# The second ring of moving tiles, laid 128 bytes further in SBUF

## The chip, the cores and the metric

The kernel runs on one core of one Trainium2 chip. The metric is the device time of one execution in microseconds (us). TensorE (PE) multiplies, VectorE (DVE) and ScalarE (ACT) work elementwise, GpSimd (POOL) does a few small steps, SyncE (SP) issues the DMAs. SBUF is the on-chip memory in which the operands lie: 128 partitions, each with its own bytes, so that a tile has a first byte within the partition.

## The reference

One layer of a decoder trunk over 2048 tokens of width 1024: a mixer of two head groups, an MLP with squared ReLU, and a gated embedding. The change touches what lies behind the mixer groups:

```python
mix = jnp.concatenate([o_a..., o_b...], axis=-1)
h = h + rms_norm(einsum('btc,cd->btd', mix, w_out), post_mix_norm)      # output projection
u = einsum('btd,df->btf', rms_norm(h, pre_mlp_norm), w_mlp_up)          # up: 1024 -> 4096
y = einsum('btf,fd->btd', square(relu(u)), w_mlp_down)                  # down: 4096 -> 1024
h = h + rms_norm(y, post_mlp_norm)
e = rms_norm(einsum('bte,ed->btd', p, w_ple_proj), ple_norm)
h = h + e * sigmoid(einsum('btd,de->bte', h, w_ple_gate))               # gate
```

All arrays are float32.

## The kernel before

**Matmuls.** Everything is held transposed: features on the partitions, tokens along them, in blocks of 512 tokens (q = 0 to 3). A float32 operand is split into two parts, high and low, of the type that TensorE reads in one pass (split, line 157: ACT copies the high part, DVE subtracts it from the original). A product takes three matmuls of 128x512 for each 128 rows: high by high, high by low, low by high. The weights, 128x128, are loaded into TensorE for each matmul; the other operand, 128x512, moves through it. So one matmul reads its moving operand from SBUF while the weights of the next are read from there.

**Stages.** Up to about 1145 us the input projection and the two mixers run (line 1020 and the lines around it). Behind them come the output projection (products named mmo, four token blocks of 8 products with 24 matmuls each), the MLP in two halves of two token blocks each (up, products named u; then down, products named d), and the gate (products named mmg). Up and down use a Strassen scheme: seven products in place of eight, with sums of tiles made by DVE. In up a group of 7 products has 12 matmuls each, 84 together, and there are 16 groups in each half. These products run through mm (line 1085) and, all but those of the down stage, through product (line 1092), which goes to the next moving tile and the next block of weights after three matmuls. The down stage (line 1540) uses one moving tile with four blocks of weights, 12 matmuls, before it goes on. Lines 1085 to 1090 also run the agenda: every 8 matmuls one step of the work that was put off (loads, splits, norms, residuals), so that this work goes with the matmuls.

**Pools.** A pool is a stretch of SBUF, cut into buffers. Pools of the left side lie one behind the other in the order in which they are opened, those of the right side from the top down. What matters here, with the buffers of each:

- left, for the whole kernel: cp (small constants), ra (10 buffers of 4096 bytes a partition), st (norms' tiles), sm (small tiles)
- left, closed before the stages behind the mixers: the mixers' pools cm, mp, m2
- left, opened in their place: pad (one tile that nothing uses), rb (18 buffers of 4096 bytes), f2 (16 buffers of 2048 bytes: results, sums and raw weights), tp (4 buffers of 2048 bytes)
- right: wp (weights: 3 buffers of 8192 and 2 of 4096 bytes), up to the first group of the up stage
- right, opened in the place of wp and tp: bp (10 buffers of 4096 bytes: weights of the up stage and the gate; both operands of the down stage)

The moving tiles of the output projection, the up stage and the gate (mixT, t, h2T) lie in the ring that ra and rb form together; next_pool deals them out. Of each 28 tiles the first 10 lie in ra, the others in rb:

```python
    def next_pool():
        turn[0] += 1
        return ra if (turn[0] - 1) % 28 < 10 else second[0]
```

Each such tile is 128 partitions by 2 parts of 512 float32, so 4096 bytes a partition; a buffer of weights has parts of 128 columns, 512 bytes. The tiles are taken in this order: mixT of token blocks 0 to 3 (8 each), 28 of the up stage's first half, 28 of its second, h2T of token blocks 0 to 3 (8 each). The moving tiles of the input projection all lie in ra, those of the down stage in bp.

Of the kernel before, what the change touches and what calls it, by code (L numbers as in the profile page):

```python
# [10 lines left out]
F32 = mybir.dt.float32  # L11
# [9 lines left out]
P = 128  # L21
# [62 lines left out]
def trunk(ctx, tc, x, xT, pT, vecs, w_in, w_ab, gdn_a_log, gdn_dt_bias, w_out, w_up, w_down,  # L84
# [986 lines left out]

    ctx.enter_context(tc.tile_pool(name="pad", bufs=1)).tile([P, 16], F32, name="pad")
    second.append(ctx.enter_context(tc.tile_pool(name="rb", bufs=18, reuse_waits="tile")))
    f2 = ctx.enter_context(tc.tile_pool(name="f2", bufs=1, reuse_waits="tile"))
    octx = ctx.enter_context(ExitStack())
# [656 lines left out]
```

## Time and profile before

| what | us |
|---|---|
| median of 3 runs | 2773.16 |
| lowest and highest | 2772.43, 2774.76 |
| profiled execution | 2769.21 |
| its span | 2767.3 |

The span runs from the first to the last instruction on the engines; the profiled execution's own time has what lies around it as well. The profile's page gives each engine's busy time, the chain of work that ended last, and groups of instructions by line, with count, busy time and mean length of one. For a stretch of time, a window gives the same busy times and counts. In order of time, a row gives the start, the length from the first to the end of the last, and the count of a run of like instructions. Matmuls overlap: one lasts some 390 ns from its first read to its last write, but the next starts well before that.

### The profile page before, as it was taken

The page shows a single profiled execution, that of the slowest core. Times are in us where ns is not written, and L with a number is a line of the kernel's source. Part 1 is how long each engine was busy: PE and PEld are TensorE (multiplying, and loading weights), DVE is VectorE, ACT ScalarE, POOL GpSimd, SP SyncE. Part 2 cuts the span into 40 slices and gives each one's busy share as a digit, 9 for nine tenths or more (in the row PEclk, how much of TensorE's full clock was granted, in tenths as well). Part 3 has the DMA queues.
Part 4 walks back from the last instruction along what each step waited for, and adds up shares of the span by engine and source line. Part 5 has one row for each costly group of instructions (what it writes and reads, how often), then busy time and mean ns, then how long its engine had stood idle before and what let it go on. Part 6 is the DMA issues. An engine that isn't in the chain of part 4 may idle for free.

```text
span 2767.3 us, 38374 instructions
## 1 busy us (share of the span) xinstructions
PE 2680.7 (97%) x12721; PEld 2215.3 (80%) x12721; DVE 2044.9 (74%) x4242; ACT 1469.9 (53%) x2943; POOL 104.2 (4%) x104
## 2 busy tenths in 40 slices
PE   6999999999999999999999999999999999999999
PEld 4788788788888887777788888887888888887887
DVE  6788877787787677578889867857787765567775
ACT  6665555455546445575555646545454445465431
POOL 0000000000000000000000000001000000001000
PEclk9999999999999999999999999999999999999999
DMA  7776777667666665887466447667454356577663
GB/s 261 255 250 217 235 247 247 219 209 250 220 213 202 214 227 170 278 276 258 140 214 224 172 175 237 225 193 239 157 191 162 135 175 203 194 254 240 214 206 121
DMA packets 268598, 589.24 MB, mean 213 GB/s; under 512 B 55642, under 2 KB 59960, under 8 KB 249200
## 3 DMA queue, kind: packets, MB, share of 16 engines
q1 hardware_dynamic: 268400, 586.79, 63.6%
q8 instruction: 101, 1.65, 0.3%
q14 instruction: 97, 0.79, 0.1%
HBM read 419.75 MB, written 166.92 MB: 212 GB/s over the span
## 4 chain that ended last, share of the span: by engine, by line
PE 61%; DVE 15%; DMA 10%; issue 7%; ACT 4%; SPq 1%; POOL 1%; DVEq 0%; POOLq 0%; ACTq 0%
PE u L1090 22%; PE d L1090 20%; PE mm L1020 9%; PE mmg L1090 6%; DVE pr_g L658 2%; DMA ud_g<-u_g 2%; DMA sys_g<-ud_g 2%; DVE xs_g L661 1%; DVE xs_g L663 1%; PE mmo L1090 1%; DMA raw_out<-in_w_out_dram 1%; DVE xt L160 1%; DMA rd_g<-m_g 1%; DMA cache_in<-w 1%; DMA rsb_g<-rd_g 1%
## 5 line engine op out<-in xcount | busy, mean ns | idle before, releaser
L1020 PE MATMUL mm<-xt,w 128*128 128x512 f32 x3072 | 770.0, 399 | 3.3 <-ACT qk_h L758 1.6
L1020 PEld LDWEIGHTS mm<-xt,w 128*128 128x128 f32 x3072 | 559.5, 189 | 109.8 <-ACT qk_h L758 2.0
L1090 PE MATMUL d<-db,da 128*128 128x512 f32 x2688 | 615.3, 391 | 5.6 <-ACT db L212 3.7
L1090 PE MATMUL u<-t,wu 128*128 128x512 f32 x2604 | 603.7, 393 | 3.3 <-ACT wu L159 3.3
L1090 PEld LDWEIGHTS d<-db,da 128*128 128x128 f32 x2688 | 506.3, 189 | 113.9 <-ACT db L212 5.0
L1090 PEld LDWEIGHTS u<-t,wu 128*128 128x128 f32 x2604 | 488.7, 188 | 117.6 <-ACT wu L159 4.1
L213 DVE TENSOR_TENSOR db<-db 128x512 fp32r<-128x512 f32 x224 | 161.4, 720 | 75.2 <-ACT db L212 74.3
L1419 DVE TENSOR_TENSOR u<-u,u 128x512 f32<-128x512 f32 x224 | 150.3, 682 | 71.8 <-PE u L1090 70.6
L212 ACT ACTIVATE db<-db 128x512 fp32r<-128x512 f32 x224 | 140.8, 629 | 83.2 <-DMA db<-hid 77.8
L1090 PE MATMUL mmo<-mixT,w_out 128*128 128x512 f32 x720 | 171.7, 399 | 8.9 <-DVE w_out L160 6.4
L1090 PE MATMUL mmg<-h2T,wg 128*128 128x512 f32 x768 | 177.4, 393 | 0.0
L1460 ACT ACTIVATE u<-u 128x512 f32<-128x512 f32 x128 | 80.8, 632 | 176.4 <-DVE u L1419 176.1
L1090 PEld LDWEIGHTS mmo<-mixT,w_out 128*128 128x128 f32 x720 | 137.1, 191 | 42.5 <-DVE w_out L160 8.2
L1090 PEld LDWEIGHTS mmg<-h2T,wg 128*128 128x128 f32 x768 | 144.2, 188 | 32.9
L160 DVE TENSOR_TENSOR da<-da 128x512 fp32r<-128x512 f32 x128 | 93.0, 727 | 87.1 <-ACT da L159 86.9
L159 ACT ACTIVATE da<-da 128x512 fp32r<-128x512 f32 x128 | 80.4, 628 | 134.9 <-DMA da<-sumd 111.3
L159 ACT ACTIVATE wu<-a 128x512 fp32r<-128x512 f32 x124 | 73.9, 622 | 50.6 <-DMA a<-in_w_up_dram 49.2
L658 DVE TENSOR_TENSOR pr_g<-xs_g,sys_g 128x16 f32<-128x16 f32 (+14 forms) x240 | 93.8, 391 | 5.3
L223 POOL TENSOR_TENSOR acc_y<-acc_y,sq_y 128x512 f32<-128x512 f32 x28 | 38.5, 1374 | 1392.8 <-ACT sq_y L222 1392.0
L160 DVE TENSOR_TENSOR wu<-a,wu 128x512 fp32r<-128x512 f32 x124 | 84.7, 686 | 3.6 <-ACT wu L159 3.5
L1461 ACT ACTIVATE u<-u 128x512 f32<-128x512 f32 x128 | 80.8, 631 | 3.7
L160 DVE TENSOR_TENSOR da<-dr,da 128x512 fp32r<-128x512 f32 x96 | 66.2, 690 | 18.5 <-ACT da L159 16.8
(374 smaller groups left out, 3800.9 us busy)
## 6 DMA issues: line engine op xcount, KB each, us to landing
w<-cache_in SPq DMA_DIRECT2D x96, 1024.0 KB
db<-hid SPq DMA_DIRECT2D x224, 256.0 KB
cache_in<-w SPq DMA_DIRECT2D x32, 1024.0 KB
hid<-u SPq DMA_DIRECT2D x128, 256.0 KB
da<-sumd SPq DMA_DIRECT2D x128, 256.0 KB
a<-in_w_up_dram SPq DMA_DIRECT2D x124, 256.0 KB
hid<-ht SPq DMA_DIRECT2D x96, 256.0 KB
dr<-in_w_down_dram SPq DMA_DIRECT2D x96, 256.0 KB
```

Source lines behind the costliest of these rows:

```text
L159: S.activation(t[:, 0], raw, AF.Copy)
L160: eng.tensor_tensor(t[:, 1], raw, t[:, 0], ALU.subtract)
L212: S.activation(t[:, 0], plain(t), AF.Copy)
L213: V.tensor_tensor(t[:, 1], plain(t), t[:, 0], ALU.subtract)
L223: eng.tensor_tensor(acc, acc, sq, ALU.add)
L658: V.tensor_tensor(pr[:, :, :, 0:i], xs[:, None, :, 0:i].broadcast_to([P, 2, GC, i]), sys[:, 0:i, i : i + 2].rearrange("p j two -> p two j" ...
L661: V.tensor_reduce(xs[:, :, i : i + 2].rearrange("p g two -> p two g"), pr[:, :, :, 0 : i + 1], AX.X, ALU.add)
L1020: PE.matmul(ps, *terms[i], start=i == 0, stop=i == nt - 1)
L1090: PE.matmul(ps, a, b, start=start, stop=stop)
L1419: V.tensor_tensor(c[new], c[old], ps, ALU.add)
L1460: S.activation(c[k], c[k], AF.Relu)
L1461: S.activation(c[k], c[k], AF.Square)
```

## The change

The tile in the pool pad, which is there only to take up room, grows from 16 to 48 float32, from 64 to 192 bytes a partition. The pools that are opened behind it on the left side, rb, f2 and tp, begin 128 bytes higher. No instruction, no order and no buffer count is changed.

```diff
@@ -1071,7 +1071,7 @@
-    ctx.enter_context(tc.tile_pool(name="pad", bufs=1)).tile([P, 16], F32, name="pad")
+    ctx.enter_context(tc.tile_pool(name="pad", bufs=1)).tile([P, 48], F32, name="pad")
     second.append(ctx.enter_context(tc.tile_pool(name="rb", bufs=18, reuse_waits="tile")))
     f2 = ctx.enter_context(tc.tile_pool(name="f2", bufs=1, reuse_waits="tile"))
     octx = ctx.enter_context(ExitStack())
```

## The prediction

> **What bounds the kernel now.** I read the page's busy shares and its chain first, then the windows of the stages behind the mixers, then the order of time of TensorE alone.
>
> ```profile
> span 2767.3 us, 38374 instructions
> ...
> PE 2680.7 (97%) x12721; PEld 2215.3 (80%) x12721; DVE 2044.9 (74%) x4242; ACT 1469.9 (53%) x2943; POOL 104.2 (4%) x104
> ...
> PE 61%; DVE 15%; DMA 10%; issue 7%; ACT 4%; SPq 1%; POOL 1%; DVEq 0%; POOLq 0%; ACTq 0%
> PE u L1090 22%; PE d L1090 20%; PE mm L1020 9%; PE mmg L1090 6%; DVE pr_g L658 2%; DMA ud_g<-u_g 2%; DMA sys_g<-ud_g 2%; DVE xs_g L661 1%; DVE xs_g L663 1%; PE mmo L1090 1%; DMA raw_out<-in_w_out_dram 1%; DVE xt L160 1%; DMA rd_g<-m_g 1%; DMA cache_in<-w 1%; DMA rsb_g<-rd_g 1%
> ```
>
> TensorE (PE) is busy for 97% and most of the chain is its matmuls of line 1090. The change touches only what is laid out behind the mixers, from about 1145 us on, so the stages from there are what counts: output projection (mmo), MLP up (u), MLP down (d), gate (mmg).
>
> ```profile
> 1145.00:1180.00 35.00, 33.94 (x149) 27.47 (x147) 14.37 (x20) 15.36 (x26) 2.02 (x2) 1.00 0.88 301
> 1180.00:1225.00 45.00, 44.84 (x192) 35.96 (x192) 36.88 (x53) 34.72 (x54) 0.00 (x0) 1.00 0.87 289
> 1225.00:1285.00 60.00, 52.37 (x209) 41.30 (x209) 49.77 (x75) 37.11 (x57) 0.00 (x0) 0.94 0.70 230
> 1285.00:1327.00 42.00, 42.00 (x184) 34.28 (x183) 34.90 (x56) 28.03 (x46) 0.00 (x0) 1.00 0.75 259
> 1327.00:1362.00 35.00, 29.37 (x113) 22.08 (x111) 23.69 (x39) 16.50 (x26) 0.00 (x0) 0.90 0.27 88
> 1362.00:1650.00 288.00, 286.78 (x1238) 232.55 (x1239) 235.21 (x379) 159.46 (x267) 0.00 (x0) 1.00 0.56 194
> ...
> 1962.00:2273.00 311.00, 310.85 (x1347) 252.40 (x1346) 231.51 (x366) 158.23 (x262) 5.83 (x4) 1.00 0.45 157
> 2273.00:2583.00 310.00, 307.57 (x1349) 253.72 (x1347) 196.55 (x293) 162.23 (x262) 13.27 (x10) 0.99 0.69 224
> 2583.00:2761.00 178.00, 178.00 (x772) 144.45 (x770) 125.11 (x191) 51.96 (x85) 5.44 (x4) 1.00 0.55 180
> ```
>
> Columns: window, length, then busy time and count of PE, its weight loads, DVE, ACT and POOL, granted clock, DMA share, GB/s. Both up stages (1362:1650, 1962:2273) and the gate (2583:2761) have TensorE busy practically without a gap at a clock of 1.00; DVE has 53 of 288 us free in the first of them. There every ns of a matmul is a ns of the kernel. From 1145 to 1362 us it isn't so: gaps, and a clock of 0.94 and 0.90.
>
> **What differs between the tiles.** Busy time hides what a matmul costs, because one is already running when the next starts. What I need is the step from start to start: (length of a gapless stretch less the last matmul's own 0.39 us) divided by (count less one). The rows below are TensorE in order of time; each is start, length, group, count.
>
> ```profile
> 1145.63 26.68 PE L1090 MATMUL mmo<-mixT,w_out 128*128 128x512 f32 x117
> 1237.10 11.08 PE L1090 MATMUL mmo<-mixT,w_out 128*128 128x512 f32 x47
> 1194.78 27.53 PE L1090 MATMUL mmo<-mixT,w_out 128*128 128x512 f32 x118
> 1292.37 28.02 PE L1090 MATMUL mmo<-mixT,w_out 128*128 128x512 f32 x121
> 1494.33 3.13 PE L1090 MATMUL u<-t,wu 128*128 128x512 f32 x13
> 1541.26 108.93 PE L1090 MATMUL u<-t,wu 128*128 128x512 f32 x470
> 2109.70 90.48 PE L1090 MATMUL u<-t,wu 128*128 128x512 f32 x391
> 2604.74 65.52 PE L1090 MATMUL mmg<-h2T,wg 128*128 128x512 f32 x283
> 2676.16 77.02 PE L1090 MATMUL mmg<-h2T,wg 128*128 128x512 f32 x334
> 1699.82 160.41 PE L1090 MATMUL d<-db,da 128*128 128x512 f32 x707
> ```
>
> Which ring a moving tile lies in follows from next_pool: of each 28 tiles taken the first 10 lie in ra, the other 18 in rb. So mixT0 is all ra (first row), mixT2 all rb (second), mixT1 is 6 of 8 rb (third), mixT3 4 of 8 (fourth). The steps:
>
> - all ra: (26.68 - 0.39) / 116 = **226.6 ns**
> - all rb: (11.08 - 0.39) / 46 = **232.4 ns**
> - 6 of 8 rb: 27.14 / 117 = 232.0 ns; 4 of 8 rb: 27.63 / 120 = 230.2 ns
> - up, first half of the tokens (18 of 28 tiles rb): 108.54 / 469 = 231.4 ns; second half: 90.09 / 390 = 231.0 ns
> - gate, token blocks 0 and 1 (10 of 16 rb): 65.13 / 282 = 231.0 ns; 2 and 3 (8 of 16): 76.63 / 333 = 230.1 ns
> - down, where moving tiles and weights both lie in bp: 160.02 / 706 = **226.7 ns**
>
> The first two are one line, one shape, weights from one pool, at full clock. So a matmul whose moving tile lies in rb costs 5.8 ns more. A mixture costs more than its share (6 of 8 should give 230.9): an rb tile also slows the next few ra matmuls. A product with 3 of its 4 tiles in ra shows it too, the fifth row: (3.13 - 0.39) / 12 = 228.3 ns.
>
> **The change part by part.** It removes and adds no instruction, wait or DMA. The pad tile grows from 64 to 192 bytes a partition, and the pools opened behind it on the left, rb, f2 and tp, lie 128 bytes higher. In the program before, the pools' sizes stack up to these first bytes: ra 18144, rb 81760, f2 155488, tp 188256, and from the right bp 188384 and wp 196576. Modulo 512 that is ra 224, rb and f2 and tp 352, bp and wp 480. A tile's parts are multiples of 512 bytes, so the residue holds for each part. The distance of the moving tile from the weights, modulo 512, is then 256 for ra (226.6 ns), 384 for rb (232.4 ns) and 0 for the down stage (226.7 ns). The change takes rb to 480, distance 0: the place of the down stage's tiles. It fits without a byte to spare: tp ends at 196448 + 128 = 196576, where wp begins, and f2 at 188256 + 128 = 188384, where bp begins. Nothing moves in wp, bp, ra, st or PSUM.
>
> *Step at distance 0.* No row shows rb there. The nearest above is the mixed product's 228.3 ns, the nearest below the pure streams' 226.6 and 226.7. I take 226.7, the row with exactly this distance and residue. With rb at 226.7 there is also nothing left that would slow the ra tiles behind it, so whole mixed streams go to 226.7.
>
> *Sum, where TensorE is the bound.*
> - up, first half: 15 of 16 groups of 84 matmuls = 1260 x (231.4 - 226.7) = 5.9 us
> - up, second half: 1344 x (231.0 - 226.7) = 5.8 us
> - gate: 384 x (231.0 - 226.7) + 384 x (230.1 - 226.7) = 1.7 + 1.3 = 3.0 us
>
> Together 14.7 us.
>
> *Output stage and first up group.* Here 192 x 5.3 + 192 x 5.7 + 192 x 3.5 = 2.8 us of steps go away, and some 0.4 us of the first up group's 84. But TensorE waits there for DVE and ACT:
>
> ```profile
> PE mmo L1090 <- DVE w_out L160: 6.4, 4, 3.1
> PE d L1090 <- ACT db L212: 3.7, 2, 2.1
> PE u L1090 <- ACT w_u L159: 3.5, 1, 3.5
> PE u L1090 <- ACT wu L159: 3.3, 2, 2.5
> PE d L1090 <- DVE db L213: 1.9, 4, 0.8
> ```
>
> (Waits of TensorE from 1145 us: total us, times, longest.) DVE is busy 49.77 of 60 us from 1225 on and 34.9 of the next 42. A TensorE that comes sooner waits longer for the same w_out, w_u and wu. I count none of these 3.2 us; the range takes them from 0 to 3.2.
>
> *Down stage.* Its step is 226.7 already and its tiles stay. Its 5.6 us of waits (db rows) hang on loads that are issued a fixed number of matmuls ahead and at the same pace; they move along. Cost 0.
>
> *DVE and ACT, whose tiles in f2 move too.* f2 comes to distance 0 from bp. Nearest rows:
>
> ```profile
> L213 DVE TENSOR_TENSOR db<-db 128x512 fp32r<-128x512 f32 x224 | 161.4, 720 | 75.2 <-ACT db L212 74.3
> L160 DVE TENSOR_TENSOR wu<-a,wu 128x512 fp32r<-128x512 f32 x124 | 84.7, 686 | 3.6 <-ACT wu L159 3.5
> L212 ACT ACTIVATE db<-db 128x512 fp32r<-128x512 f32 x224 | 140.8, 629 | 83.2 <-DMA db<-hid 77.8
> L159 ACT ACTIVATE wu<-a 128x512 fp32r<-128x512 f32 x124 | 73.9, 622 | 50.6 <-DMA a<-in_w_up_dram 49.2
> ```
>
> db lies with both operands and its result in bp (distance 0), wu takes one operand from f2 (distance 128 from bp). At most a subtraction becomes 34 ns longer, 7 in a group of some 19.4 us (84 x 231.4): 0.24 us of DVE's free 3.6 us (53 of 288). Likelier nothing. Either way TensorE's matmuls hide it in the up stage; without that cover it would be 32 groups x 0.24 = 7.6 us. In the output stage, where DVE is late, the split w_out stays inside wp.
>
> *Reuse of old memory.* rb, f2 and tp lie where the mixers' pools lay, and a tile waits for the old ones under it. By the addresses each new tile has, shifted, the same last old user beneath it, and the load of rb's first tile is issued only about here in the chain:
>
> ```profile
> 1164.06 4.36 DMA mixT<-mixd
> ```
>
> That is 19 us into the output stage (1145), whose products no longer read a mixer's tile. Cost 0.
>
> The profiled execution took 2769.21 us, 1.9 beside its span of 2767.3, and 2769.21 - 14.7 = 2754.5. The median of the runs is 2773.16, 4 us above it; the stages are the same, so I take the same difference: **2773.16 - 14.7 = 2758.5 us**, 0.53% faster.
>
> **Rivals.**
>
> *Half of it.* Streams that alternate between distance 0 and ra's 256 might not settle as the pure ones do. The mixed product's 228.3 ns is the row for that. Then up gains 1260 x 3.1 + 1344 x 2.7 = 7.5 us, the gate 384 x 2.7 + 384 x 1.8 = 1.7: 9.2 us, 2764.0. For it: only pure streams are seen at 226.7. Against it: the extra steps follow rb tiles, and those are cured first.
>
> *The distance is not what matters.* rb could be slow for where it lies in SBUF, or for what is read beside it, and the change does nothing: 2773.2. For it: residue, region and pool change together between the rows, so none is isolated. Against it: rb's region lies between ra's and bp's, both at 226.7 or below, and rb is slow in three stages with different neighbours.
> The Trainium skill speaks for this rival: its page "SBUF — State Buffer", section "Who interferes with whom", gives TensorE two independent read ports, one for the moving operand and one for the weights, and says "PE and ACT never wait on anyone". By that rule no distance matters and the time stays at 2773.2. The 226.6 against 232.4 ns of the same line are nothing that the rule explains, which is why I leave it a small chance only.
>
> *Slower.* The down stage keeps one moving tile for 12 matmuls; products of line 1092 change it every 3, together with the weights. Two streams at distance 0 that advance together could then meet more often, not never. The durations give the price:
>
> ```profile
> L1090 PE MATMUL mmo<-mixT,w_out x47: 390/393/404, 1237.1 to 1247.8; 128*128 128x512 f32 x47
> ```
>
> (All rb: min, median, max ns.) If each rb matmul took the longest form, 404 in place of 393, 11 ns more, the 54 of 84 in 31 up groups and the 432 of the gate, 2106 together, cost 23 us: 2796. It decides from the point where the step at distance 0 is above 232.4 ns. Against it: ra changes its tile every 3 too, at 226.6.
>
> **How the numbers follow.** A measurement of this kernel can tell about 0.2%, 5.5 us, from no change. Forecast (14.7 us and what the output stage adds): 0.62, its own range 2754 to 2762. Half of it: 0.18, 2760 to 2768. Nothing: 0.13. Slower: 0.07. So faster 0.80, within 0.2% 0.13, slower 0.07. The low end is 2773.16 - 14.7 - 3.2 = 2755.3, less the 0.7 us by which the lowest run (2772.43) lies below its median: 2754. The high end is that of half, with only some 5 us gained, 2768; what is left out, no change and slower, is 2 in 10.
>
> **What would show it.** In the profile after: all rb (mixT2) at 226.7 ns a step; up from 231.4 and 231.0 and the gate from 231.0 and 230.1 to the same; d unchanged. The groups of the page have means that rb raises too:
>
> ```profile
> L1090 PE MATMUL u<-t,wu 128*128 128x512 f32 x2604 | 603.7, 393 | 3.3 <-ACT wu L159 3.3
> L1090 PE MATMUL mmg<-h2T,wg 128*128 128x512 f32 x768 | 177.4, 393 | 0.0
> ```
>
> Both should fall from 393 to about 389 ns. Each up stage is about 6 us shorter, the gate 3, the down stages as before. Waits for w_out, w_u and wu together grow by up to 3 us. Wrong if mixT2 stays at 232 (the distance is not it), if it falls and the mixed streams stay at 228 (half), if the step rises (slower), or if the steps fall and new waits for wu, db or wg take the gain: then another engine was closer than 53 us in 288 suggests.

## The result and the profile after

The changed kernel takes 2761.45 us, median of 5 runs (2754.01 to 2763.47), against 2773.16 (2772.23 to 2774.76) before. The ratio is 0.9948, 95% interval 0.9936 to 0.9959: faster by 0.41 to 0.64%. The forecast was 2758.5, a ratio of 0.9947. The profiled execution is the slowest of the five, 2763.47 us.

The page of the changed kernel first, TensorE's share and its four groups of line 1090 (busy us, mean ns of one, idle before):

```profile
span 2761.6 us, 38372 instructions
...
PE 2672.5 (97%) x12721; PEld 2219.0 (80%) x12721; DVE 2045.6 (74%) x4242; ACT 1469.3 (53%) x2943; POOL 104.4 (4%) x104
...
L1090 PE MATMUL d<-db,da 128*128 128x512 f32 x2688 | 617.2, 391 | 6.9 <-ACT db L212 4.9
...
L1090 PE MATMUL u<-t,wu 128*128 128x512 f32 x2604 | 593.3, 390 | 3.5 <-ACT wu L159 3.4
...
L1090 PE MATMUL mmo<-mixT,w_out 128*128 128x512 f32 x720 | 169.2, 395 | 9.6 <-DVE w_out L160 7.1
L1090 PE MATMUL mmg<-h2T,wg 128*128 128x512 f32 x768 | 174.5, 389 | 0.0
```

The means of u and mmg have gone from 393 to 390 and 389 ns, that of d is 391 as before. DVE and ACT have the same counts and within 1 us the same busy time. The page alone cannot say more, since matmuls overlap. The steps can: the same kernel, TensorE in order of time (start, length, group, count), in the order of the prediction's rows: mixT0, mixT2, mixT1, mixT3, up in both halves, gate in both halves, down.

```profile
1151.81 22.38 PE L1090 MATMUL mmo<-mixT,w_out 128*128 128x512 f32 x98
1240.55 13.31 PE L1090 MATMUL mmo<-mixT,w_out 128*128 128x512 f32 x58
1198.70 23.51 PE L1090 MATMUL mmo<-mixT,w_out 128*128 128x512 f32 x103
1295.70 22.60 PE L1090 MATMUL mmo<-mixT,w_out 128*128 128x512 f32 x99
1560.71 79.50 PE L1090 MATMUL u<-t,wu 128*128 128x512 f32 x350
2119.70 70.66 PE L1090 MATMUL u<-t,wu 128*128 128x512 f32 x311
2609.80 50.48 PE L1090 MATMUL mmg<-h2T,wg 128*128 128x512 f32 x222
2689.81 50.48 PE L1090 MATMUL mmg<-h2T,wg 128*128 128x512 f32 x222
1699.74 160.64 PE L1090 MATMUL d<-db,da 128*128 128x512 f32 x708
```

With 0.39 us off for the last matmul, the steps are 226.7, 226.7, 226.7, 226.6, 226.7, 226.7, 226.7, 226.7 and 226.7 ns. Before they were 226.6, 232.4, 232.0, 230.2, 231.4, 231.0, 231.0, 230.1 and 226.7. Every stream, pure or mixed, is now at the step that ra's and the down stage's had.

Where that arrives is read from the first and last start of a group. Each row below has min/median/max ns of one and the starts of the first and the last matmul. Before the change:

```profile
L1090 PE MATMUL mmo<-mixT,w_out x720: 387/392/632, 1145.4 to 1327.1; 128*128 128x512 f32 x180
L1090 PE MATMUL mmg<-h2T,wg x768: 387/392/404, 2583.2 to 2760.8; 128*128 128x512 f32 x192
```

After it:

```profile
L1090 PE MATMUL mmo<-mixT,w_out x720: 387/389/628, 1150.0 to 1329.9; 128*128 128x512 f32 x180
L1090 PE MATMUL mmg<-h2T,wg x768: 387/389/402, 2580.5 to 2755.1; 128*128 128x512 f32 x192
```

From the first output matmul of line 1090 to the last gate matmul it took 2760.8 - 1145.4 = 1615.4 us, and takes 1605.1: 10.3 less. But this stretch began 4.6 us later, behind mixers that the change does not touch. So the spans of the two profiled executions differ by only 5.7 us. The waits of TensorE behind the mixers, after (total us, times, longest):

```profile
PE mmo L1090 <- DVE w_out L160: 7.1, 4, 3.1
PE d L1090 <- ACT db L212: 4.9, 3, 2.1
PE u L1090 <- ACT w_u L159: 4.2, 1, 4.2
PE u L1090 <- ACT wu L159: 3.4, 2, 2.6
```

Those for w_out, w_u and wu were 6.4, 3.5 and 3.3: 1.5 us more together. That for db was 3.7. Two things were open: whether the distance is the cause, and whether the later start and the longer waits belong to the change or to the execution.

### The profile page after: what moved, and what is told of

Its sections match the earlier page's. It is cut to its first block, busy times and chain, and to the rows that moved or that the text cites. A ratio compares the mean times of both kernels' runs of the same rounds, so it can differ in the third digit from the quotient of the medians.

```text
span 2761.6 us, 38372 instructions
## 1 busy us (share of the span) xinstructions
PE 2672.5 (97%) x12721; PEld 2219.0 (80%) x12721; DVE 2045.6 (74%) x4242; ACT 1469.3 (53%) x2943; POOL 104.4 (4%) x104
## 4 chain that ended last, share of the span: by engine, by line
PE 57%; DVE 9%; DMA 6%; issue 5%; ACT 3%; POOL 1%; SPq 1%; DVEq 0%; POOLq 0%; ACTq 0%
PE u L1090 21%; PE d L1090 20%; PE mmg L1090 6%; PE mm L1020 6%; DVE pr_g L658 1%; DMA ud_g<-u_g 1%; DMA sys_g<-ud_g 1%; PE mmo L1090 1%; DVE xs_g L661 1%; DMA rd_g<-m_g 1%; DMA rsb_g<-rd_g 1%; DMA raw_out<-in_w_out_dram 1%; DVE xs_g L663 1%; DMA db<-hid 1%; DMA mixT<-mixd 0%
## 5 line engine op out<-in xcount | busy, mean ns | idle before, releaser
L1090 PE MATMUL u<-t,wu 128*128 128x512 f32 x2604 | 593.3, 390 | 3.5 <-ACT wu L159 3.4
```

The lines of the kernel that those rows point to most:

```text
L1090: PE.matmul(ps, a, b, start=start, stop=stop)
```

## The experiments

The theory: the distance of the moving tile from the weights, as first bytes in a partition modulo 512, sets the step. Its rivals: the moving tile's own residue, the ring's region in SBUF, or f2 and tp, which the change moves as well. Every edit is shown against the kernel before. Experiments that were measured side by side share the runs of the kernel before.

### f2 and tp moved, rb left

```diff
     second.append(ctx.enter_context(tc.tile_pool(name="rb", bufs=18, reuse_waits="tile")))
+    ctx.enter_context(tc.tile_pool(name="pad2", bufs=1)).tile([P, 32], F32, name="pad2")
     f2 = ctx.enter_context(tc.tile_pool(name="f2", bufs=1, reuse_waits="tile"))
```

> rb stays 384 bytes (modulo 512) from the weights; f2 and tp alone lie 128 bytes higher, as in the changed kernel. If the distance of the moving tile from the weights sets the step of a matmul, mixT2 stays at 232.4 ns a step, the up stages at 231.4 and 231.0, and the time is that before, 2773. If it was f2's place that counted (f2 now at distance 0 from bp), the steps fall to 226.7 and the time to that of the changed kernel, 2761.

The time is 2775.17 us (10 runs) against 2775.64 (25 runs), ratio 0.9999 (0.9988 to 1.001). mixT2 in order of time:

```profile
1249.92 13.70 PE L1091 MATMUL mmo<-mixT,w_out 128*128 128x512 f32 x58
```

13.31 / 57 = 233.5 ns. It is slow as before, where the same 58 matmuls took 13.64 us, 232.5 ns a step. The 1 ns between the two, with rb at the same distance, shows how far a slow step differs from one profile to the next. And the first and last starts:

```profile
L1091 PE MATMUL mmo<-mixT,w_out x720: 387/392/632, 1158.0 to 1340.0; 128*128 128x512 f32 x180
L1091 PE MATMUL mmg<-h2T,wg x768: 387/392/398, 2596.5 to 2773.9; 128*128 128x512 f32 x192
```

The stretch is 1615.9 us, half a us from the kernel before. f2 and tp have no part in it. The stretch begins at 1158.0, 12.6 us later than in the profile before, with nothing changed ahead of it: the mixers' time differs that much between profiles.

### The weights moved, the rings left

```diff
+    ctx.enter_context(tc.tile_pool(name="wpad", bufs=1, side="right")).tile([P, 32], F32, name="wpad")
     wctx = ctx.enter_context(ExitStack())
     wp = wctx.enter_context(tc.tile_pool(name="wp", bufs=3, side="right"))
```

> All rings stay where they were before; the weights' pools wp and bp lie 128 bytes lower. rb is then at distance 0 from the weights with its old residue 352, ra at distance 384 with its old residue 224. If the distance counts, mixT2 falls to 226.7 ns a step and mixT0 rises from 226.6 to some 232.4; the input projection, 3168 matmuls from ra, takes up to 3168 x 5.8 = 18 us more, less what its waits cover, and the stages behind it gain about 8 of the 17 us in which rb was slow: about 2783. If the moving tile's own residue counts (352 slow, 224 and 480 fast), both steps stay, and the time is 2773.

The time is 2771.83 us (10 runs), ratio 0.9987 (0.9977 to 0.9996). mixT0, then mixT2:

```profile
1157.63 17.59 PE L1091 MATMUL mmo<-mixT,w_out 128*128 128x512 f32 x75
1246.28 13.31 PE L1091 MATMUL mmo<-mixT,w_out 128*128 128x512 f32 x58
```

17.20 / 74 = 232.4 ns for ra, 12.92 / 57 = 226.7 for rb. No tile of ra or rb has changed its place, and the two rings have changed their parts. So it is not the tile's own residue and not its region but the distance. The steps came out as expected, the time did not: 2772 and not 2783. The input projection shows why:

```profile
L1021 PE MATMUL mm<-xt,w 128*128 128x512 f32 x3072 | 781.8, 403 | 2.8 <-DVE acc_vg L503 1.8 <-ACT zt_zg L538 0.7 <-ACT qk_h L759 0.2
```

Before, this group was busy for 770.0 us with a mean of 399 ns, so it grew by 12 us and not by 18. The stretch behind it begins here:

```profile
L1091 PE MATMUL mmo<-mixT,w_out x720: 387/390/796, 1153.9 to 1336.4; 128*128 128x512 f32 x180
L1091 PE MATMUL mmg<-h2T,wg x768: 387/389/404, 2587.8 to 2764.7; 128*128 128x512 f32 x192
```

1153.9 us is within what kernels with a fast ra show (1140.6 to 1158.0), so of the 12 us little is seen in the time. That the mixers' waits take it up is likely, and was not tried by itself. From there it is 1610.8 us, 4.6 less than before, where 8 were expected.

### rb as changed, ra moved to distance 384

```diff
+    ctx.enter_context(tc.tile_pool(name="pad0", bufs=1)).tile([P, 32], F32, name="pad0")
     ra = ctx.enter_context(tc.tile_pool(name="ra", bufs=10))
```

> rb at distance 0 as in the changed kernel, ra 128 bytes higher, at distance 384 and residue 352. If distance or residue counts, and not the ring's region in SBUF, mixT0 rises to 232.4 ns, mixT2 is 226.7, and the time is about 2783, as with the weights moved. If a region is slow and rb was cured by something else, mixT0 stays at 226.6 and the time is 2761.

The time is 2773.32 us (10 runs), ratio 0.9989 (0.9978 to 1.0001). mixT0 and mixT2:

```profile
1157.72 17.59 PE L1091 MATMUL mmo<-mixT,w_out 128*128 128x512 f32 x75
1246.10 13.32 PE L1091 MATMUL mmo<-mixT,w_out 128*128 128x512 f32 x58
```

232.4 ns for ra, 226.8 for rb: at 384 either ring is slow. The time missed 2783 as with the weights moved, and again the gain is that of the stretch behind the mixers: by its first and last start (1153.5 and 2766.5) it is 1613.0 us, 2.4 less than before, and the median is 2.3 less.

### The changed kernel again

> The changed kernel again, for a second profile. Steps of 226.7 ns in mixT2, up and gate as in the first. If the 2 and 1.6 us by which its down stages, and the 4.6 us by which its mixers were longer in the first profile are chance, they differ here by as much in either direction; if the change brings them, the down stages are again 313.6 and 311.4 us or more. Time 2754 to 2764.

The time is 2759.71 us (4 runs) against 2775.64, ratio 0.9944 (0.9925 to 0.9963).

```profile
L1090 PE MATMUL mmo<-mixT,w_out x720: 387/389/797, 1154.2 to 1335.0; 128*128 128x512 f32 x180
L1090 PE MATMUL mmg<-h2T,wg x768: 388/389/398, 2582.8 to 2757.5; 128*128 128x512 f32 x192
```

That is 1603.3 us behind the mixers, 12.1 less than before. By the starts of the first matmul of each stage its down stages took 312.5 and 308.8 us, where the first profile had 313.6 and 311.4 and the kernel before 311.6 and 309.8. They differ in either direction, so the longer down stages of the first profile do not belong to the change.

### Seven other distances

To make room for any distance, one tile of 512 bytes (rows) goes to a pool that is closed with the mixers, and pad takes the size that puts rb where it is wanted. ra stays at 256. For distance 128:

```diff
-    rows = cp.tile([N_ROWS, P], F32, name="rows")
+    rows = cm.tile([N_ROWS, P], F32, name="rows")
...
-    ctx.enter_context(tc.tile_pool(name="pad", bufs=1)).tile([P, 16], F32, name="pad")
+    ctx.enter_context(tc.tile_pool(name="pad", bufs=1)).tile([P, 80], F32, name="pad")
```

The pad has 56, 64, 80, 112, 32 and 40 columns for distances 32, 64, 128, 256, 448 and 480; for 320 the line is left out.

> rb at distance 128 from the weights, modulo 512 (rows moved out of cp to make room; ra stays at 256). If only the distance modulo 256 counts (0 and 256 fast, 384 slow), 128 is slow as 384 is: mixT2 at 232.4 ns a step. If there is a zone of slow distances around 384, mixT2 is at 226.7.

> rb at distance 64. If the distance modulo 256 counts, 64 lies between a fast 0 and a slow 128: between 226.7 and 232.4 ns or at one of them. If there is a zone around 384, 226.7.

> rb at distance 320, between the fast 256 and the slow 384. If there is a zone around 384 that is wider than 64 bytes to either side, mixT2 is at or near 232.4 ns a step here; if modulo 256 counts, the same step as at distance 64.

> rb at distance 448, between the slow 384 and the fast 0. Zone around 384 that is symmetric: the same step as at 320. Modulo 256: the same as at 192, not run here; between 226.7 and 232.4.

> rb at distance 32. If the step rises evenly from 0 to 128 (226.7, 229.7 at 64, 232.8), about 228.2 ns in mixT2; if any distance other than a multiple of 256 is slow, 229 or more.

> rb at distance 480, 32 bytes short of 512. At 448 the step was 233.4 ns. If the step falls evenly from there to 0, about 230 ns in mixT2; if a multiple of 256 is a narrow good place, 232 or more.

> rb at distance 256, the same as ra (rows moved out of cp to make room). The runs so far gave 229.7 and 229.1 ns at 64 and 320, 232.8 and 232.5 at 128 and 384: if only the distance modulo 256 counts, mixT2 is at 226.7 here, the up stages at 226.7 and the time is that of the changed kernel, some 2760. If rb needs a multiple of 512, or lies in a slow region, mixT2 stays above 229.

The same 58 matmuls of mixT2 in each, in order of time (start, length, group, count). Distance 32 first, then 64, 128, 256, 320, 448 and 480, one row each:

```profile
1236.85 13.69 PE L1090 MATMUL mmo<-mixT,w_out 128*128 128x512 f32 x58
```

```profile
1239.76 13.45 PE L1090 MATMUL mmo<-mixT,w_out 128*128 128x512 f32 x58
```

```profile
1240.74 13.64 PE L1090 MATMUL mmo<-mixT,w_out 128*128 128x512 f32 x58
```

```profile
1236.99 13.31 PE L1090 MATMUL mmo<-mixT,w_out 128*128 128x512 f32 x58
```

```profile
1241.18 13.44 PE L1089 MATMUL mmo<-mixT,w_out 128*128 128x512 f32 x58
```

```profile
1244.19 13.69 PE L1090 MATMUL mmo<-mixT,w_out 128*128 128x512 f32 x58
```

```profile
1234.65 13.69 PE L1090 MATMUL mmo<-mixT,w_out 128*128 128x512 f32 x58
```

All have the same count, so the lengths compare directly. As steps, beside those of the kernels above:

| distance | modulo 256 | step, ns | time, us: median of the changed kernel, 256 and 384, else a single run |
|---|---|---|---|
| 0 (changed kernel) | 0 | 226.7 | 2761.45, 2759.71 |
| 256 | 0 | 226.7 | 2752.84 |
| 32 | 32 | 233.3 | 2770.75 |
| 64 | 64 | 229.1 | 2773.94 |
| 320 | 64 | 228.9 | 2774.96 |
| 128 | 128 | 232.5 | 2774.71 |
| 384 (kernel before) | 128 | 232.5; 233.5 with f2 and tp moved | 2773.16; 2775.17 |
| 448 | 192 | 233.3 | 2780.4 |
| 480 | 224 | 233.3 | 2769.41 |

The times are from different chips and are not to be compared with each other. The steps are: 0 and 256 agree, 64 and 320 agree within 0.2 ns, and 128 agrees with one of the two profiles at 384. As those two are 1 ns apart, 232.5 and 233.3 cannot be told from each other here, but 226.7, 229 and 232.5 can. Only the multiples of 256 reach 226.7. There is no zone around 384, and no even rise from 0 to 128 either: 32 bytes off the good place cost 6.6 ns, more than 64 do. The expectation of an evenly growing cost for 32 and 480 failed; that of a narrow good place held.

At distance 256 the kernel takes 2752.84 us (4 runs) against 2769.94 (8 runs), ratio 0.9939 (0.9923 to 0.9955), and behind the mixers the starts are

```profile
L1090 PE MATMUL mmo<-mixT,w_out x720: 387/389/793, 1147.7 to 1327.5; 128*128 128x512 f32 x180
L1090 PE MATMUL mmg<-h2T,wg x768: 388/389/397, 2572.7 to 2747.4; 128*128 128x512 f32 x192
```

That is 1599.7 us. The ratio's interval overlaps that of the changed kernel: a distance of 256 does what 0 does.

### Both rings at distance 0

```diff
+    ctx.enter_context(tc.tile_pool(name="pad0", bufs=1)).tile([P, 64], F32, name="pad0")
     ra = ctx.enter_context(tc.tile_pool(name="ra", bufs=10))
...
-    ctx.enter_context(tc.tile_pool(name="pad", bufs=1)).tile([P, 16], F32, name="pad")
+    ctx.enter_context(tc.tile_pool(name="pad", bufs=1)).tile([P, 112], F32, name="pad")
```

(rows in cm, as above.)

> Both rings at distance 0: ra moved by 256 bytes, rb as in the changed kernel. Modulo 256: nothing to gain, input projection matmuls stay at a mean step of 228.75 ns, time about 2760. Modulo 512: ra's matmuls in the input projection fall toward 226.7, up to 3072 x 2 = 6 us less, about 2754.

The time is 2753.86 us (5 runs), ratio 0.9950 (0.9932 to 0.9968), no better than distance 256, which was measured beside it. The input projection:

```profile
L1021 PE MATMUL mm<-xt,w 128*128 128x512 f32 x3072 | 772.2, 400 | 1.9 <-ACT qk_h L759 1.2 <-ACT zt_zg L538 0.7
```

772.2 us busy against 770.0 before: ra gains nothing from 0 in place of 256, as modulo 256 says. From start to start these matmuls take 228.3 ns on average in both profiles, a little under the 228.75 of the expectation. Behind the mixers:

```profile
L1091 PE MATMUL mmo<-mixT,w_out x720: 387/389/796, 1140.6 to 1320.6; 128*128 128x512 f32 x180
L1091 PE MATMUL mmg<-h2T,wg x768: 388/389/398, 2564.2 to 2739.0; 128*128 128x512 f32 x192
```

That is 1598.4 us.

## Why the prediction was right

*The step at distance 0* was taken as 226.7 ns from the down stage, whose tiles have that distance and residue. It is 226.7 in every stream. The rival "half" falls with it: mixed streams settle too. The runs show why they can: ra at 256 and rb at 0 are the same place modulo 256, so no alternation is left. The prediction had the two as different distances that both happen to be fast; the right statement is one distance, modulo 256.

*The sum of 14.7 us* was made behind the mixers, and there it is found. The four profiles with all rings at a multiple of 256 (1605.1, 1603.3, 1599.7, 1598.4) have a mean of 1601.6 us. The two with rb at 384 and ra at 256 have 1615.4 and 1615.9. That is 14.0 less, though over different chips. Two of these profiles were taken side by side, the one with f2 and tp moved and the second of the changed kernel; they differ by 12.6. The medians fell by 11.7, 15.9, 17.1 and 16.1 us. The first two profiles show only 10.3 behind the mixers, and 5.7 in the spans, because the mixers of the second took 4.6 us longer. The start of the output stage lies between 1140.6 and 1158.0 us in kernels whose code ahead of it is the same but for an offset that keeps the distance modulo 256, and it is not the change that moves it: with rb at 0 or 256 it lies between 1140.6 and 1154.2, with rb slow between 1142.9 and 1158.0. It accounts for most of the spread among the four profiles with all rings at a multiple of 256, whose spans go from 2745.5 to 2764.0.

By the starts of the first matmul of each stage, those four profiles against those two, the places are not all as counted:

| stage | forecast, us | found, us |
|---|---|---|
| output | 0 (2.8 left to the range) | 1.7 |
| up, first half | 5.9 (0.4 more left to the range) | 4.3 |
| up, second half | 5.8 | 5.6 |
| gate | 3.0 | 2.8 |
| down, both | 0 | -0.4 |

In the first half every group of 84 without a norm's matmuls takes 19.04 us in place of 19.43 from the third on, the 0.39 that 84 x 4.7 ns gives. What is missing lies in the first two groups. They took 50.2 us before and 51.9 after. The wait for w_u grew by 0.7, and behind the wait for wu TensorE ran at half the clock in the first profile after the change, and at the full one before. These two rows are windows behind that wait, with the columns of the prediction, before first: 28 matmuls in 6.8 us at a granted clock of 1.00, then 7 in 3.1 us at 0.50.

```profile
1363.20:1370.00 6.80, 6.78 (x28) 5.25 (x29) 6.80 (x13) 4.84 (x9) 0.00 (x0) 1.00 0.63 230
```

```profile
1366.90:1370.00 3.10, 3.10 (x7) 2.39 (x8) 3.10 (x6) 3.10 (x7) 0.00 (x0) 0.50 0.81 264
```

Whether the change brings the slow clock is not shown. Matmuls at 427 ns a step stand behind this wait in three of the four profiles with all rings fast, not in the one with both rings at 0, and at the slow distances 64, 128 and 320 as well.

So the steps were forecast rightly. That the total of 14.0 comes so near to 14.7 is in part luck, because the output stage's 1.7, which was not counted, makes up for what the first half lacks.

*The output stage*, of which nothing was counted, gave 1.7 of its 2.8 us of steps. In the first profile TensorE waits there 0.7 us longer for w_out.

*Down stage, DVE and ACT, reuse of memory* were put at nothing. The step of the down stage is 226.7 in both, the DVE and ACT totals differ by less than 1 us, and f2 and tp moved alone change nothing (0.9999).

*The rival by which distance does not matter* falls with the weights moved: no tile of ra or rb was moved and the two rings changed their steps. The page "SBUF — State Buffer" of the Trainium skill, section "Who interferes with whom", says that TensorE never waits on anyone and has two independent read ports. What the runs show is that its two own reads, moving tile and weights, are not independent of each other's addresses: 226.7 ns at multiples of 256 bytes, 228.9 to 233.5 at the others tried. Whether the two meet in a part of the memory or in TensorE's own path, no run here tells.

*The rival by which it becomes slower* needed a step above 232.4 at distance 0, and falls with 226.7.

What failed beyond that was outside the prediction: the expectations of 2783 us for a slow ra. They priced the input projection's matmuls at the pure streams' 5.8 ns and as if most of it reached the end. From start to start these matmuls went from 228.3 ns on average to 232.6, so by 4.3; the group grew by 12 us, not 18, and of those little was seen. Behind the mixers 8 us were expected and 4.6 and 2.4 came: with 10 of 28 tiles slow the up stages stepped at 230.1 and 229.9, where shares of 232.4 and 226.7 would give 228.7.

## What to carry to other kernels

Where TensorE is busy without a gap, work out the step from start to start for each source of its moving operand, since the busy time and the mean length of one show it poorly (393 against 390 ns here). If the same shape steps differently, compare first bytes: moving tile against weights, modulo 256 here. A pad that makes them agree costs no instruction, but it has to be counted again whenever a pool ahead of it changes its size.

## What was not expected of the hardware

In the pairs tried (0 and 256, 64 and 320, 128 and 384) the step goes by the distance modulo 256, and among the nine distances it is fast only on the multiples (226.7 ns); at 32, 64, 128, 192 and 224 it is 233.3, 229.1, 232.5, 233.3 and 233.3, where 232.5 and 233.3 lie within the 1 ns by which two profiles at 384 differ. A slow matmul also slows the next ones of a fast tile: in the kernel before, up groups with 18 of 28 tiles slow stepped at 231.4, where shares of 232.4 and 226.6 would give 230.3. The starts show it directly in mixT3 of that kernel, whose products go through four rb tiles and then four ra tiles: on average the first ra tile still stepped at 231.7 ns, the three behind it at 226.7. And a ring at 64 or 320 is no cheaper as a whole than one at 128, in spite of its own 229: at 320 the starts behind the mixers are

```profile
L1089 PE MATMUL mmo<-mixT,w_out x720: 387/392/795, 1150.3 to 1332.4; 128*128 128x512 f32 x180
L1089 PE MATMUL mmg<-h2T,wg x768: 387/392/398, 2590.1 to 2766.6; 128*128 128x512 f32 x192
```

That is 1616.3 us, as slow as at 384; at 64 and 128 it is 1616.7 and 1616.3.
